# Which early store goes out in two halves of 64 partitions: row 1's, or that of rows 2 and 3

## The chip, the cores and the metric

The kernel runs on one core of a Trainium2 chip. The metric is device time in microseconds (us); a lower time is better. Differences under 2% count as "same". The profile is of one execution; its span, from the first to the last instruction, is about 1.7 us shorter than the timed run.

## The reference

Batch normalization with running statistics, then ReLU, on 32 x 128 x 32 x 32 float32 numbers, 16.78 MB in and 16.78 MB out:

```python
normalized = (x - running_mean[None, :, None, None]) / np.sqrt(running_var[None, :, None, None] + eps)
scaled = normalized * gamma[None, :, None, None] + beta[None, :, None, None]
return np.maximum(scaled, 0).astype(np.float32)
```

## The kernel before

The tensor is cut into two blocks t of 128 partitions x 16 rows x 1024 numbers; a row is one channel image of 4 KB in each partition. SyncE issues the six loads, ScalarE (ACT) computes each row in place with one activation (the first three rows of the second block with two), and issues the stores itself.

```python
TILES = ((0, 0, 2), (0, 2, 4), (0, 4, 16), (1, 0, 16))
LOAD_CUTS = {(0, 8), (1, 8)}
STORE_CUTS = {(0, 1)}
TWO_PARTS = {(0, 1)}
...
nc.sync.dma_start(out=xt[:, c - a : d - a, :], in_=xr[t, :, c:d, :])
...                                            # parameters: scale_t, bias_t
for t, a, b, xt in tiles:
    first = a
    for j in range(a, b):
        ...                                    # activation(s) of row j, Relu(scale * x + bias)
        if j + 1 == b or (t, j + 1) in STORE_CUTS:
            parts = P // 2 if (t, j) in TWO_PARTS else P
            for p in range(0, P, parts):
                nc.scalar.dma_start(out=outr[t, p : p + parts, first : j + 1, :],
                                    in_=xt[p : p + parts, first - a : j + 1 - a, :])
            first = j + 1
```

In order: row 0 (512 KB), row 1 in two halves (256 KB each), rows 2 and 3 (1 MB), rows 4 to 15 (6 MB), the second block (8 MB).

## Time and profile before

| | before |
|---|---|
| time, median of 3 runs | 83.4 us (83.33 to 83.64) |
| span of the profiled run | 81.7 us |
| ScalarE busy | 39.3 us (48%) |
| load queue q1 / store queue q10, share of 16 DMA engines | 48.6% / 47.7% |

Read the two shares first: they are packet time, that is, time in which a DMA engine moves a piece (packet) of a transfer, and they leave 3.7% of the span for everything that isn't a transfer. The prediction shows the lines.

### The profile page before, as it was taken

Reading aid. Unit: us, or ns where it says so; the run is one execution under the profiler, and the core shown is the slowest. Engines: PE = TensorE matmul, PEld = TensorE weight load, DVE = VectorE, ACT = ScalarE, POOL = GpSimd, SP = SyncE. Lnnn points to the kernel's source line nnn. Section 1 sums busy time; section 2 is a strip of 40 time slices with the busy share of each in tenths; the row PEclk is TensorE's granted clock in tenths of the full one; section 3 lists DMA queues with packets and bytes.
Section 4 is the critical chain, followed back from the end, with each engine's and each line's share of the span. In section 5 each row is a group of like instructions: output and inputs, shape, how many; then the busy total and the mean of one; then the engine's idle time right before and its main releaser. Section 6 shows DMA issues by size and latency. Waiting matters only on the chain.

```text
span 81.7 us, 129 instructions
## 1 busy us (share of the span) xinstructions
PE 1.8 (2%) x6; PEld 1.5 (2%) x6; DVE 0.8 (1%) x5; ACT 39.3 (48%) x37; POOL 0.8 (1%) x6
## 2 busy tenths in 40 slices
PE   0007000000000000000000000000000000000000
PEld 0016000000000000000000000000000000000000
DVE  0003000000000000000000000000000000000000
ACT  0601658797039999199998099994000000000000
POOL 3000000000000000000000000000000000000000
DMA  1999998898989799979789988889992899999290
GB/s 40 361 421 461 425 537 353 377 489 377 489 343 523 343 491 411 487 293 589 337 361 601 513 385 385 385 385 409 625 633 128 385 513 513 513 513 417 96 513 0
DMA packets 1665, 33.56 MB, mean 411 GB/s; under 512 B 257, under 2 KB 257, under 8 KB 513
## 3 DMA queue, kind: packets, MB, share of 16 engines
q1 hardware_dynamic: 864, 16.78, 48.6%
q10 hardware_dynamic: 800, 16.78, 47.7%
q14 instruction: 1, 0.00, 0.0%
HBM read 16.78 MB, written 16.78 MB: 411 GB/s over the span
## 4 chain that ended last, share of the span: by engine, by line
DMA 55%; ACT 10%; issue 2%; SPq 1%
DMA x<-in_x_dram 55%; ACT x L113 10%; SPq L58 1%
## 5 line engine op out<-in xcount | busy, mean ns | idle before, releaser
L113 ACT ACTIVATE x<-x,bias_t,scale_t 128x1024 f32<-128x1024 f32 (+1 forms) x35 | 37.8, 1154 | 11.4 <-DMA x<-in_x_dram 7.7
L95 ACT ACT_TABLE_LOAD x1 | 1.3, 1283 | 2.6 <-issue 2.6
L86 PE MATMUL cols<-raw,rep 8*128 8x16 f32 (+1 forms) x6 | 1.8, 384 | 6.3 <-DMA raw<-in_gamma_dram 6.0
L86 PEld LDWEIGHTS cols<-raw,rep 8*128 8x128 f32 x6 | 1.5, 306 | 6.5 <-issue 5.9
L95 ACT ACTIVATE std_t<-cols,eps_t 128x16 f32<-128x16 f32 x1 | 0.3, 273 | 2.7 <-PE cols L86 2.7
L72 POOL TENSOR_SCALAR_AFFINE_SELECT rep<-rep 8x128 f32<-8x128 f32 x1 | 0.4, 393 | 0.1
L99 DVE RECIPROCAL rstd_t<-std_t 128x16 f32<-128x16 f32 x1 | 0.3, 252 | 6.0 <-ACT std_t L95 6.0
L71 POOL MEMSET rep<- 8x128 f32 x1 | 0.2, 194 | 0.3 <-POOLq L144 0.3
L105 DVE TENSOR_TENSOR bias_t<-cols,ms_t 128x16 f32<-128x16 f32 x1 | 0.2, 175 | 0.4 <-PE cols L86 0.4
L103 DVE TENSOR_TENSOR ms_t<-cols,scale_t 128x16 f32<-128x16 f32 x1 | 0.2, 176 | 0.1
L101 DVE TENSOR_TENSOR scale_t<-cols,rstd_t 128x16 f32<-128x16 f32 x1 | 0.2, 175 | 0.1
L144 POOL MEMSET const-bfloat16-1.0<- 128x1 bf16 x1 | 0.1, 106 | 0.0
L144 POOL MEMSET const-uint8-127<- 128x1 uint8 x1 | 0.1, 106 | 0.0
L144 POOL MEMSET const-float32-0.0<- 128x1 f32 x1 | 0.1, 103 | 0.3 <-issue 0.3
L144 POOL MEMSET const-float32-1.0<- 128x1 f32 x1 | 0.1, 103 | 0.0
L69 DVE MEMSET eps_t<- 128x1 f32 x1 | 0.1, 59 | 0.9 <-PEq L144 0.9
## 6 DMA issues: line engine op xcount, KB each, us to landing
x<-in_x_dram SPq DMA_DIRECT2D x3, 4096.0 KB, 34.1
out_dram<-x ACTq DMA_DIRECT2D x1, 6144.0 KB, 28.5
x<-in_x_dram SPq DMA_DIRECT2D x2, 1024.0 KB, 5.6
x<-in_x_dram SPq DMA_DIRECT2D x1, 2048.0 KB, 11.1
out_dram<-x ACTq DMA_DIRECT2D x1, 1024.0 KB
out_dram<-x ACTq DMA_DIRECT2D x1, 512.0 KB, 14.4
out_dram<-x ACTq DMA_DIRECT2D x2, 256.0 KB, 19.2
raw<-in_running_var_dram ACTq DMA_DIRECT2D x1, 0.5 KB
```

The lines of the kernel that those rows point to most:

```text
L58: nc.sync.dma_start(out=xt[:, c - a : d - a, :], in_=xr[t, :, c:d, :])
L69: nc.vector.memset(eps_t, float(eps))
L71: nc.gpsimd.memset(rep, 1.0)
L72: nc.gpsimd.affine_select(out=rep, in_=rep, compare_op=mybir.AluOpType.is_equal, fill=0.0, base=0, pattern=[[0, P // Q], [-1, Q]], channel ...
L86: nc.tensor.matmul(c.rearrange("p k j -> p (k j)"), rep.rearrange("q r s -> q (r s)"), raw[a].rearrange("q k j -> q (k j)"), start=True, s ...
L95: nc.scalar.activation(out=std_t, in_=cols[0][:, 0, :], func=ACTF.Sqrt, bias=eps_t[:, 0:1], scale=1.0)
L99: nc.vector.reciprocal(out=rstd_t, in_=std_t)
L101: nc.vector.tensor_mul(out=scale_t, in0=cols[0][:, 1, :], in1=rstd_t)
L103: nc.vector.tensor_mul(out=ms_t, in0=cols[1][:, 0, :], in1=scale_t)
L105: nc.vector.tensor_sub(out=bias_t, in0=cols[2][:, 0, :], in1=ms_t)
L113: nc.scalar.activation(out=xt[:, j - a, w : w + step], in_=xt[:, j - a, w : w + step], func=ACTF.Relu, bias=bias_t[:, j : j + 1], scale=sc ...
L144: nc = _bacc.Bacc("TRN2", target_bir_lowering=False, num_devices=1)
```

## The change

The intent is to issue row 1 with one instruction, so that ScalarE comes to row 2 sooner, and to keep the number of transfers by splitting the next store.

```diff
-TWO_PARTS = {(0, 1)}
+TWO_PARTS = {(0, 3)}
```

## The prediction

> **What bounds the kernel now.** I read the page first, for which engine is full. ScalarE (ACT) does all the visible arithmetic and is busy for 48% of the span; TensorE, VectorE and GpSimd do next to nothing. The DMA engines are the ones with no holes.
>
> ```profile
> span 81.7 us, 129 instructions
> ...
> ACT  0601658797039999199998099994000000000000
> ...
> DMA  1999998898989799979789988889992899999290
> ...
> q1 hardware_dynamic: 864, 16.78, 48.6%
> q10 hardware_dynamic: 800, 16.78, 47.7%
> ...
> HBM read 16.78 MB, written 16.78 MB: 411 GB/s over the span
> ```
>
> Queue q1 carries the loads that SyncE issues, q10 the stores (and the tiny parameter loads) that ScalarE issues. Each percentage is packet time as a share of 16 engines over the span. Together they are 96.3%, and 0.963 x 81.7 = 78.7 us. The packet records of the trace (start, size and duration of each packet) begin at 1.8 us and the last one ends at 80.6 us, a stretch of 78.8 us. So an average engine stands still for about 0.1 us between its first packet and its last. The single digits below 9 in the DMA row come from packets being as long as a slice (one 32 KB packet takes 1.21 us, a slice is 2.04 us), not from idleness; a table of windows confirms it (columns: length of the stretch, five engines' busy times, clock, DMA share, GB/s):
>
> ```profile
> 13.00:24.00 11.00, 0.00 (x0) 0.00 (x0) 0.00 (x0) 6.65 (x7) 0.00 (x0) 1.00 1.01 429
> 24.00:36.00 12.00, 0.00 (x0) 0.00 (x0) 0.00 (x0) 10.31 (x10) 0.00 (x0) 1.00 1.03 437
> 36.00:46.00 10.00, 0.00 (x0) 0.00 (x0) 0.00 (x0) 8.71 (x10) 0.00 (x0) 1.00 0.94 404
> ```
>
> Row 0's store moves in the first of these, the two halves of row 1 in the second, rows 2 and 3 in the third. The shares (a packet is counted whole where it starts, so 1.03 and 0.94 are the same thing) average 1.00.
>
> Third, the chain that ended last. Its view stops at 56 us, because ScalarE's last instruction is its end; what comes after is seen in the waits of SyncE's queue, which sits through the stores until the program ends:
>
> ```profile
> SPq L158 <- DMA out_dram<-x: 67.6, 3, 34.0
> SPq L58 <- DMA x<-in_x_dram: 5.0, 1, 5.0
> SPq L58 <- DMA raw<-in_beta_dram: 4.7, 1, 4.7
> ```
>
> The last store's completion arrives at 80.9 us, then 0.8 us of closing. The other 1.7 us up to the 83.4 us of the timed runs lie outside the profiled span. So the kernel is 33.56 MB through 16 engines that are never idle, plus 4.6 us of fixed ends (1.8 before the first packet, 0.3 from the last packet to its completion, 0.8, and 1.7). Only a change in bytes, in time per byte, or in idle engine time can move it.
>
> Fourth, the timeline of ScalarE around the stores concerned (start, length, what; in brackets the engine's idle time before it):
>
> ```profile
> 9.60 0.39 ACTq L123 DMA_DIRECT2D out_dram<-x  x1
> 10.03 1.24 ACT L113 ACTIVATE x<-x,bias_t,scale_t 128x1024 f32<-128x1024 f32 x1 [0.46 <-ACT x L113]
> 11.30 1.18 ACTq L123 DMA_DIRECT2D out_dram<-x  x2
> 12.53 2.37 ACT L113 ACTIVATE x<-x,bias_t,scale_t 128x1024 f32<-128x1024 f32 x2 [1.26 <-issue]
> 14.93 0.38 ACTq L123 DMA_DIRECT2D out_dram<-x  x1
> 15.35 4.63 ACT L113 ACTIVATE x<-x,bias_t,scale_t 128x1024 f32<-128x1024 f32 x4 [0.46 <-ACT x L113]
> 23.88 9.16 ACT L113 ACTIVATE x<-x,bias_t,scale_t 128x1024 f32<-128x1024 f32 x8 [3.90 <-DMA x<-in_x_dram]
> ```
>
> Row 1's two issues take 1.18 us against 0.39 and 0.38 for a whole one. After row 7, at 19.98 us, ScalarE waits 3.90 us for the load of rows 8 to 15.
>
> **What the Trainium skill says.** "DMA: Bandwidth & Descriptors", Rules for kernel authors, says of two transfers to disjoint partition halves "Don't bother — they serialize"; the trace agrees: row 1's halves land at 30.5 and 36.1 us, one after the other. The same page, Queues, rings and completion order, says that each DMA engine takes turns between the queues that have work, a packet at a time. The packet records agree exactly: a 32 KB load packet of 1.213 us alternates with one store packet, 0.159 us for 4 KB or 0.309 us for 8 KB, and a 4-byte completion write takes a turn of its own. The page "SBUF — State Buffer", Door 1: The DMA port swizzle, says that 64 adjacent partitions reach only half of the 16 ports, at 196 GB/s against 328 for 128. That would speak against halves, but the trace doesn't show it here: in the packet records the 4 KB packets of row 1's halves take 159 ns, those of the whole row 0 take 159 to 160 on average. "Perfetto Trace Analysis", Roofline, puts a single core's ceiling at about 435 GB/s of its 16 engines; the trace has 33.56 MB in 78.8 us = 426 GB/s. There is no slack to win.
>
> **The change part by part.** The name in the code is the last row of a store, so row 1 (the transfer of 512 KB) becomes one of 128 partitions, and rows 2 and 3 (1024 KB) become two of 64 partitions with 8 KB each.
>
> Removed: one issue at row 1. Two take 1.18 us, one about 0.38, so row 2 starts near 11.30 + 0.42 = 11.7 us instead of 12.53, 0.8 us earlier; its load landed at 7.9 us, so nothing else holds it.
> Added: one issue after row 3, again about 1.18 in place of 0.38 us. Rows 2 and 3 end at 11.7 + 2.4 = 14.1, the issues at 15.3, and row 4 starts at 15.3 to 15.4 us, against 15.35 now. The two cancel. If they didn't, the 3.90 us wait before row 8 would take it up.
> DMA packets: row 1 stays 128 packets of 4 KB, 8 an engine (two times 4 before); rows 2 and 3 stay 128 of 8 KB, 8 an engine. The number of transfers stays six, so completion writes stay six times 16. Bytes, packet sizes and packets: change 0.
> Order in the store queue: an engine's turns are now 8+1 (row 0), 4+1 and 4+1 (row 1), 8+1 (rows 2 and 3), that is 28. They become 9, 9, 5, 5: again 28, beside the same load packets. Row 1 no longer spends a turn on a completion in its middle, so its end and the start of rows 2 and 3 come one load packet earlier: first 8 KB packets near 35.4 instead of 36.6 us. The completion between the halves gives the turn back, about 41.5 us. When the last load packet ends (46.4 us), seven of the eight 8 KB packets of an engine have gone, before and after. The load of the first rows of the second block (landing 34.7 us) may meet one more 4 KB packet: 0.16 us later, and ScalarE, which ends that block at 44.7 us, has 2.15 us of wait after it. So the last load still lands near 46.8, ScalarE ends near 56.0, and the last store is issued at 56.05 while the store before it is still moving until 61.2 us.
> Sum: 0.8 - 0.8 on ScalarE, off the path; 0.00 us on the DMA engines. Predicted 83.4 us.
>
> **The rivals.** First, crowded ports: if an 8 KB packet of a half took twice its time, eight packets an engine at 0.309 us more would add 2.5 us, 85.9 us in all (+3%). For it speaks the SBUF page; against it row 1's 159 ns. Only a small trace of it could be there: the load packets beside the first packets of row 1's second half take some 1.28 instead of 1.213 us, once per engine, under 0.1 us, and similar ones stand where no half begins.
> Second, completion semaphores: transfers share them in turn, which is why the SyncE queue waits 5.0 us (its last load waits for the load of rows 4 to 7). If the change shifted who shares with whom, a load might be held back. Against: the count of transfers, and row 1 now one fewer and rows 2 and 3 one more, leaves all later ones at their places; and the load queue has 8 MB before it at that point, so even a wait until row 0's store has landed (24.0 us) would starve nothing: 83.4 still.
> Third, an earlier ScalarE: starting row 2 0.8 us sooner might bring stores sooner and gain. Against: the store queue of each engine is backed up from 13.3 us on (row 0's packets move until 24 us), so an earlier issue only waits longer: 83.4.
> Fourth, a wobble in how the two queues interlock: the load packets' excess over 1.213 us sums to about 0.33 us an engine (29.46 us of packet time for 24 x 1.213 = 29.11). Redistributing it could give plus or minus 0.15 us.
>
> **Range and chances.** The three runs spread from 83.33 to 83.64. With that and the fourth rival, 83.15 to 83.75 should hold it 8 times in 10. A change of 2% is 1.7 us; only the first rival makes one, and the trace contradicts it for 4 KB packets; I leave 1.5% for it and half a percent for a gain that I don't see.
>
> **What would show it.** In the profile after: the two queues' packets still 864 and 800 with shares summing to 96 to 97%; row 2 starting near 11.7 and row 4 near 15.35 us; an issue pair of about 1.2 us after row 3; 8 KB packets still 0.309 us, the first near 35.4; last load landing 46.8, last store's completion 80.9 us. The prediction would be wrong if 8 KB packets of the halves took longer than 0.4 us, if a load stood behind a semaphore until the load queue was empty, or if the DMA share fell below 1 in a stretch between 13 and 80 us.

## The result, and the profile after

The changed kernel took 83.69 us (83.46 to 83.72, 6 runs) against 83.53 us (83.33 to 83.73, 6 runs) for the kernel before. The ratio is 1.0015, 95% interval 0.9995 to 1.0034: the same. A ratio here is the mean time of one kernel's fast runs over that of the other's of the same rounds, so it is not quite the ratio of the medians.

Lines of the page of the changed kernel that answer to those of before:

```profile
span 81.9 us, 129 instructions
...
DMA  2899999997979797979979988889997599999190
...
q1 hardware_dynamic: 864, 16.78, 48.5%
q10 hardware_dynamic: 800, 16.78, 47.6%
...
HBM read 16.78 MB, written 16.78 MB: 410 GB/s over the span
```

The packet counts and bytes of both queues are those of before, and the shares are within 0.1 point. By the packet records an average engine works for 78.76 us, against 78.67 us before, and stands still for 0.2 us between its first and last packet, against 0.1 us. The windows of the changed kernel (length, busy times of five engines, clock, DMA share, GB/s) say that the engines stay full through the stretches in which the early stores go out:

```profile
13.00:24.00 11.00, 0.00 (x0) 0.00 (x0) 0.00 (x0) 5.82 (x6) 0.00 (x0) 1.00 1.01 429
24.00:36.00 12.00, 0.00 (x0) 0.00 (x0) 0.00 (x0) 10.19 (x10) 0.00 (x0) 1.00 1.03 440
36.00:46.00 10.00, 0.00 (x0) 0.00 (x0) 0.00 (x0) 8.96 (x10) 0.00 (x0) 1.00 0.93 401
```

The timeline of the changed kernel around the edit (start, length, what, and in brackets the idle time before it):

```profile
8.21 0.33 SPq L58 DMA_DIRECT2D x<-in_x_dram  x1
...
11.39 0.37 ACTq L123 DMA_DIRECT2D out_dram<-x  x1
11.81 2.37 ACT L113 ACTIVATE x<-x,bias_t,scale_t 128x1024 f32<-128x1024 f32 x2 [0.45 <-ACT x L113]
14.21 1.18 ACTq L123 DMA_DIRECT2D out_dram<-x  x2
15.44 4.63 ACT L113 ACTIVATE x<-x,bias_t,scale_t 128x1024 f32<-128x1024 f32 x4 [1.26 <-issue]
24.06 9.16 ACT L113 ACTIVATE x<-x,bias_t,scale_t 128x1024 f32<-128x1024 f32 x8 [3.98 <-DMA x<-in_x_dram]
```

The 1.18 us pair of issues has moved from after row 1 to after row 3. Row 2 starts 0.72 us earlier, row 4 0.09 us later, and the wait before row 8 is what it was. The first line is a surprise: SyncE's last load goes out at 8.21 us, not at 12.77. The waits of SyncE's queue say why:

```profile
SPq L158 <- DMA out_dram<-x: 72.3, 3, 38.7
SPq L58 <- DMA raw<-in_beta_dram: 4.6, 1, 4.6
...
SPq L58 <- DMA x<-in_x_dram: 0.4, 1, 0.4
```

The 5.0 us wait of before is down to 0.4 us: the last load now waits for the load of rows 2 and 3 (landed at 8.19 us), no longer for that of rows 4 to 7. The transfers share eight completion semaphores, counters that tell the issuing engine that a transfer has landed; a transfer is issued only when the one that had its semaphore before has landed. With the edit the assignment changed, though the number of transfers did not: the last load and the 6 MB store swapped semaphores. Why the program's builder chose so, no run shows.

The span is 0.18 us longer in this one profile. At least part of that isn't of the change: the load of rows 0 and 1 already lands at 5.70 us in place of 5.38, before the first altered instruction.

### The profile page after: what moved, and what is told of

The parts are those of the page before. It is cut to its first block, busy times and chain, and to the rows that moved or that the text cites. A ratio compares the mean times of both kernels' runs of the same rounds, so it can differ in the third digit from the quotient of the medians.

```text
span 81.9 us, 129 instructions
## 1 busy us (share of the span) xinstructions
PE 1.7 (2%) x6; PEld 1.5 (2%) x6; DVE 0.8 (1%) x5; ACT 39.3 (48%) x37; POOL 0.8 (1%) x6
## 2 busy tenths in 40 slices
DMA packets 1664, 33.56 MB, mean 410 GB/s; under 512 B 256, under 2 KB 256, under 8 KB 512
## 4 chain that ended last, share of the span: by engine, by line
DMA 56%; ACT 10%; issue 2%; SPq 0%
DMA x<-in_x_dram 56%; ACT x L113 10%; SPq L58 0%
```

## The experiments

The theory: all 33.56 MB go through 16 DMA engines that are always busy; the edit alters neither bytes nor packets nor idle time, so neither the issues on ScalarE nor the place of the halves matter. The rivals: a half costs something of its own; ScalarE's issue time is on the path; the earlier last load hides a cost. Twelve runs were made, one of them a repeat of the changed kernel; all gave correct results. Times are medians; the kernel before ran beside them in each of three calls at 83.74, 83.55 and 83.73 us. By the 2% rule most of these runs are "the same"; the intervals of several leave out 1 all the same, and these small differences are discussed as such.

| run | edit | time us | ratio to before, 95% |
|---|---|---|---|
| after_again | the changed kernel | 83.62 | 0.999 (0.9975 to 1.0006) |
| no_halves | no store in halves | 84.30 | 1.007 (1.0053 to 1.0086) |
| both_halves | row 1 and rows 2 and 3 | 83.98 | 1.0043 (1.002 to 1.0066) |
| last_halves | row 1 and the last store | 103.40 | 1.2355 (1.2335 to 1.2374) |
| quarters | rows 2 and 3 in four | 84.07 | 1.0057 (1.0027 to 1.0087) |
| eighths | rows 2 and 3 in eight | 93.41 | 1.1179 (1.1148 to 1.1211) |
| busy_in_row2 | 5 us more ScalarE work early | 83.53 | 0.9997 (0.9979 to 1.0015) |
| busy_at_end | 10 us more ScalarE work late | 89.80 | 1.0751 (1.0724 to 1.0777) |
| row0_halves | row 0 alone in halves | 83.88 | 1.0023 (1.0007 to 1.0039) |
| rows01_halves | rows 0 and 1 in halves | 84.38 | 1.008 (1.0062 to 1.0099) |
| single_rows | no halves, rows 2 and 3 singly | 84.34 | 1.0076 (1.0061 to 1.0092) |
| pairs_whole | no halves, rows 0 and 1 in one | 92.89 | 1.1099 (1.1081 to 1.1117) |

**after_again.** No edit to the changed kernel; five rounds.

> The changed kernel unaltered, timed in five rounds, since 0.16 us lay between the medians and the interval touched 1. Theory (16 DMA engines always busy, same packets before and after, so no difference): ratio within 0.998 to 1.002 of before. Rival (a small real cost of the halves of rows 2 and 3, about 0.15 us): ratio 1.001 to 1.003 with an interval that leaves out 1.

Measured 83.62 us, ratio 0.999. With the first ratio of 1.0015 on the other side of 1, the theory's interval holds and no cost of 0.15 us is seen.

**no_halves, both_halves.** Against the kernel before:

```diff
-TWO_PARTS = {(0, 1)}
+TWO_PARTS = set()                 # no_halves
+TWO_PARTS = {(0, 1), (0, 3)}      # both_halves
```

> No store in halves: row 1 and rows 2 and 3 whole, one transfer and 16 completion writes fewer. Theory: 83.5 us, within 0.2 us of before; ScalarE issues 0.8 us less and only waits longer before row 8. Rival 1 (a half costs something): 0.15 us or more faster than the changed kernel. Rival 2 (ScalarE's issue time is on the path): 0.8 us faster.

> Row 1 and rows 2 and 3 both in halves: ScalarE issues 0.8 us more than either kernel, and the last load again shares a completion semaphore with the load of rows 4 to 7 (issued near 13 us, as in the kernel before, not near 8 us as in the changed one). Theory: 83.6 us, within 0.2 us of both. Rival 1 (halves cost): 0.15 us above the changed kernel. Rival 3 (the earlier issue of the last load in the changed kernel hid a cost of the halves): here the cost would come out, 0.3 us or more above the kernel before.

The theory missed both: 0.7% and 0.4% slower than before, where it said equal. Alone, both_halves would fit a cost of the halves (0.36 us above after_again) or a hidden one. But no_halves contradicts every rival: with less issue time, one transfer fewer and no half at all, it should have been equal or faster, and it is the slowest of the three. In both_halves the last load again waits until 12.75 us, as in the kernel before; but since no_halves is slow with an early last load (7.82 us), and the kernel before is fast with a late one, the time of that issue isn't what hides or makes a cost. Where the time went is taken up below, with the runs that were meant to explain it.

**last_halves.** The kernel before, with its last store in halves too.

```diff
-TWO_PARTS = {(0, 1)}
+TWO_PARTS = {(0, 1), (1, 15)}
```

> The kernel before with its last store of 8 MB in halves of 64 partitions as well. It moves alone at the end, so nothing hides what a half costs: this measures the disputed cost by itself. Theory (an engine's rate is its own, whatever partitions it reads): 64 KB packets stay 2.42 us, 83.6 us in all. Rival (64 partitions reach half of the ports): packets take about 4.8 us, eight an engine, so 19 us more, 103 us; then the halves of rows 2 and 3 were harmless only for being short and between load packets.

The rival hit: 103.4 us. Windows over the last store, first of the kernel before, then of this one (the last two figures are the DMA share and GB/s):

```profile
61.00:80.00 19.00, 0.00 (x0) 0.00 (x0) 0.00 (x0) 0.00 (x0) 0.00 (x0) 1.00 0.96 417
```

```profile
61.00:80.00 19.00, 0.00 (x0) 0.00 (x0) 0.00 (x0) 0.00 (x0) 0.00 (x0) 1.00 0.91 193
80.00:100.00 20.00, 0.00 (x0) 0.00 (x0) 0.00 (x0) 0.00 (x0) 0.00 (x0) 1.00 0.98 210
```

The engines are as busy as before and move half. In the packet records a 64 KB packet takes 5.11 us (median) in place of 2.418. A busy share alone can't tell a full engine from one that is held up; the GB/s beside it can. So a half of 64 partitions does cost double in a store of 8 MB that moves alone. In the changed kernel it doesn't: its 8 KB packets take 0.309 us, as in the kernel before, apart from four of the last 16, which come when the loads are ending and take 0.33 to 0.488 us. An engine's 8 KB packets add up to 2.50 us, against 2.47 us before.

**quarters, eighths.** The changed kernel with finer parts:

```diff
-parts = P // 2 if (t, j) in TWO_PARTS else P
+parts = P // 4 if (t, j) in TWO_PARTS else P     # quarters
+parts = P // 8 if (t, j) in TWO_PARTS else P     # eighths
```

> Rows 2 and 3 in four transfers of 32 partitions: twice the splits, 1.2 us more issue time than the changed kernel, and the last load now shares a completion semaphore with row 0's store, so it can't be issued before that lands at 24 us. Theory: the load queue holds work until 34 us and ScalarE's wait before row 8 shrinks from 4.0 to about 2.8 us, so 83.6 us, within 0.25 us of before. Rival (issue time or the shared semaphore on the path): 1.2 us more or beyond.

> Rows 2 and 3 in eight transfers of 16 partitions. Now the transfers share semaphores with stores that are still waiting in the queue: ScalarE can't issue the seventh before row 1's store has landed (35 us) nor the eighth before the second has, so rows 4 to 15 start near 37 us, and the last load must wait for the first eighth. Theory (only idle DMA engines cost time): engines stand idle between about 47 and 52 us and again before the last store, which is issued near 70 us; 93 us, 91 to 96. Rival (splits cost nothing whatever their number): 83.7 us.

In quarters the last load could not go out before 24.96 us, when row 0's store had landed, and still landed at 46.73 us. The wait cost nothing at the load. The time is 0.57% up, more than the 0.25 us expected and less than the rival's 1.2 us; it is one of the small misses treated below, where it stays unexplained for the most part. Eighths came out as expected, 93.4 us. Its timeline and its windows:

```profile
14.31 22.34 ACTq L123 DMA_DIRECT2D out_dram<-x  x8
36.70 13.68 ACT L113 ACTIVATE x<-x,bias_t,scale_t 128x1024 f32<-128x1024 f32 x12 [22.42 <-DMA out_dram<-x]
```

```profile
46.00:53.00 7.00, 0.00 (x0) 0.00 (x0) 0.00 (x0) 6.56 (x8) 0.00 (x0) 1.00 0.54 229
...
67.00:72.00 5.00, 0.00 (x0) 0.00 (x0) 0.00 (x0) 2.85 (x3) 0.00 (x0) 1.00 0.49 210
```

Eight issues take 22.34 us, because the fifth needs a semaphore that row 0's store holds until 24.8 us, and the seventh one that row 1's store holds until 35.8 us. ScalarE is held until 36.7 us, and the DMA share then falls to about a half twice. The shared semaphores of the prediction's second rival are a real cost, once the wait outlasts the queue.

**busy_in_row2, busy_at_end.** The changed kernel with idle work on ScalarE, four activations into a spare tile after row 2, or eight after row 14 of the second block:

```diff
+if (t, j) == (0, 2):              # busy_at_end: (1, 14), range(8)
+    for _ in range(4):
+        nc.scalar.activation(out=spare, in_=xt[:, j - a, :], func=ACTF.Relu, ...)
```

> The changed kernel with four more activations into a spare tile between rows 2 and 3, about 4.7 us of ScalarE work, six times what a split's issue costs. Theory: rows 4 to 7 end near 24.8 us, 0.8 us past the landing of the next load, and the wait near 35 us takes that up; 83.65 us, within 0.25 us of the changed kernel. Rival (ScalarE early in the kernel is on the path): up to 4.7 us more.

> The changed kernel with eight more activations before its last row, about 9.2 us, so that the last store is issued near 65.4 us instead of 56.2. Theory: the store before it drains at 61.4 us; the engines then stand idle until about 1 us after the issue, 66.4 us, so 5 us more, 88.7 us (88 to 89.5). This shows how much late ScalarE work is free: about 4 us. Rival (all ScalarE work is off the path): 83.7 us; rival (all of it is on the path): 92.9 us.

The early work, 5.06 us by the trace, is free: 83.53 us. The wait before row 8 is gone and the one near 35 us is 0.66 us, so nearly all slack there is used, and the time doesn't notice:

```profile
13.14 5.06 ACT L123 ACTIVATE spare<-x,bias_t,scale_t 128x1024 f32<-128x1024 f32 x4
...
34.93 1.52 ACT L114 ACTIVATE x<-x,bias_t,scale_t 128x512 f32<-128x512 f32 x2 [0.66 <-DMA x<-in_x_dram]
```

The late work took 10.15 us, a little more than I counted on (1.27 us an activation in place of 1.15), and cost 89.8 - 83.6 = 6.2 us. The time lies above the expected range of 88 to 89.5 us, mostly because the added work was longer; 10.15 - 6.2 = 4.0 us of it were free, as expected. The window of busy_at_end in which the engines wait for the last store, which is issued at 66.34 us:

```profile
61.00:66.50 5.50, 0.00 (x0) 0.00 (x0) 0.00 (x0) 5.21 (x5) 0.00 (x0) 1.00 0.00 0
```

A DMA share of 0.00 is what a cost on the path looks like in this kernel.

**row0_halves, rows01_halves, single_rows, pairs_whole.** These were to explain the 0.4 to 0.7% of no_halves and both_halves. My second theory was the number of turns that an engine takes in the store queue before the 6 MB store: 28 in the kernels before and after, 27, 29 and 30 in the slower ones.

```diff
-STORE_CUTS = {(0, 1)}
-TWO_PARTS = {(0, 1)}
+STORE_CUTS = {(0, 1)};          TWO_PARTS = {(0, 0)}             # row0_halves
+STORE_CUTS = {(0, 1)};          TWO_PARTS = {(0, 0), (0, 1)}     # rows01_halves
+STORE_CUTS = {(0, 1), (0, 3)};  TWO_PARTS = set()                # single_rows
+STORE_CUTS = set();             TWO_PARTS = set()                # pairs_whole
```

> Only row 0 in halves. The runs without halves (27 turns of each engine in the store queue before the 6 MB store), with both pairs (29) and with quarters (30) were 0.3 to 0.7% slower than before, the kernels before and after (28) were equal. Theory: what counts is the number of turns, not which row has the halves; here 28 again: ratio to before 0.998 to 1.002, about 83.6 us. Rival (the row matters): 0.3% or more off.

> Rows 0 and 1 in halves, rows 2 and 3 whole: 29 turns, like the run with row 1 and rows 2 and 3 in halves. Theory of the number of turns: ratio 1.003 to 1.006, about 84.0 us, and load packets near 43 us that take longer than 1.213 us. Rival (the halves of 8 KB packets made that run slower): ratio 0.998 to 1.002.

> No halves, but rows 2 and 3 in a store each of 4 KB packets: four early stores, 36 turns of 4 KB, so the loads end some 0.6 us earlier (near 46.1 us) and nine turns of row 3's store are left after them. If the slowness without halves came from the 48 KB packets of the next store standing close behind the last load packet, it must be gone here: ratio 0.998 to 1.002, about 83.6 us. If 28 is the only good number of turns: ratio 1.003 or more. If it came from having no halves at all: ratio 1.005 or more.

> No halves and rows 0 and 1 in one store like rows 2 and 3: 18 turns. The early stores are then through near 41 us, so the 48 KB packets of the 6 MB store come between the last four load packets (1.815 us each in place of 0.309): the last load lands near 54 us in place of 46.8, ScalarE ends near 63 us, the engines wait about 3 us for the last store, and the time is 86.9 us (86 to 88). Rival (only bytes count, in whatever order they go): 83.5 us.

Row0_halves has 28 turns and is 0.23% slower, with an interval that leaves out 1; rows01_halves has 29 turns and is at 0.8%, above its range; single_rows, with 36 turns, is at 0.76%, so the 48 KB packets behind the last load packet aren't the cause either; the two alternatives named there would fit, but both_halves and row0_halves are slow with halves, and row0_halves with 28 turns. The number of turns doesn't order these results: 28 turns gave 0.9990, 0.9997 and 1.0023 at the same number, and 29 gave 1.0043 and 1.008. That theory falls as I put it.

What the packet records do show is where most of the time sits. Per engine, the 24 load packets of 32 KB add up to:

| | before | after | after_again | no_halves | both_halves | row0_halves | rows01_halves | single_rows |
|---|---|---|---|---|---|---|---|---|
| us | 29.46 | 29.37 | 29.52 | 29.99 | 29.80 | 29.93 | 30.05 | 30.13 |
| above before | | -0.09 | 0.06 | 0.53 | 0.34 | 0.47 | 0.59 | 0.67 |

For no_halves, 0.53 us stand against (1.007 - 1) x 83.7 = 0.59 us in the timed runs; for both_halves 0.34 against 0.36; for single_rows 0.67 against 0.64. (One profile each; for row0_halves the profile has more than the timed 0.19 us.) The store packets' time moves by less than 0.1 us an engine among these runs, and the engines' idle time between first and last packet is 0.0 to 0.2 us in all of them. In no_halves, rows01_halves, row0_halves and single_rows most of it is in the last load packet of each engine: 1.35 to 2.0 us in place of 1.213. In the kernel before, the last load packets take 1.213 us; in the two profiles of the changed kernel one and three of the 16 take 1.28 to 1.375 us. In both_halves the longer packets are spread over the loading (0.15 us of their excess lie after 41 us).

Two things don't fit this account. Quarters is 0.49 us slower by its mean time, but its load packets take only 29.64 us, 0.18 above before. And part of the loss lies outside the profiled span: timed run less span is 1.73 us on average in the kernels before and after, but 1.88 us in no_halves, 1.90 in both_halves, 1.93 in rows01_halves and 1.85 in quarters. So these variants lose little in issue, in semaphores or in idle engines; for the most part load packets take longer. What stretches them, and what the rest is, stays open.

Pairs_whole was expected at 86.9 and came to 92.9 us. Its timeline after the loads, and the window in which the engines then stand idle:

```profile
60.13 9.16 ACT L113 ACTIVATE x<-x,bias_t,scale_t 128x1024 f32<-128x1024 f32 x8 [12.96 <-DMA x<-in_x_dram]
69.32 0.34 ACTq L123 DMA_DIRECT2D out_dram<-x  x1
```

```profile
61.00:64.00 3.00, 0.00 (x0) 0.00 (x0) 0.00 (x0) 3.00 (x4) 0.00 (x0) 1.00 0.00 0
```

The early stores landed by 38.7 us, not near 41; from there each load packet took turns with a 48 KB packet of 1.815 us. Six load packets of an engine and the load's completion write were still to come, (59.75 - 38.5) / (1.213 + 1.815) = 7 turns, where I had counted four load packets. The last load landed near 60.1 us and ScalarE's last rows had nothing to run beside. So order can matter after all: the small early store packets keep the large ones from coming between the loads. The edit in question leaves that guard as it is: eight 4 KB packets and eight of 8 KB for rows 1 to 3 on each engine, and three completions.

No run beat both kernels.

## Why the prediction was right

The time, 83.69 and later 83.62 us, lies in the range of 83.15 to 83.75, and "same" is what came. That it was so close is in part luck: the same reasoning gave 83.5 us for no_halves, which took 84.30, and nothing in the prediction tells the one edit from the other. What is shown is the bound and that the moved issues are free; "within 0.3 us" isn't.

*Bound.* Right. Only runs in which the DMA engines stood idle (busy_at_end, eighths, pairs_whole) or were held up (last_halves) lost more than 1%. Early ScalarE work of 5.06 us cost nothing.

*ScalarE's part.* Right within 0.1 us: row 2 at 11.81 us (predicted near 11.7), row 4 at 15.44 (15.3 to 15.4), pair of issues 1.18 us (about 1.18).

*Packets and turns.* Right: 864 and 800 packets; the first 8 KB packet at 35.43 us (35.4), the completion writes between the halves from 41.50 us on (about 41.5); the last load landed at 46.97 and in the second profile at 46.81 us (46.8), the last store's completion came at 81.09 and 80.99 us (80.9).

*Second rival, semaphores.* The step "leaves all later ones at their places" was wrong. The number of transfers stayed, but the builder's order did not, and the last load went out 4.56 us earlier. The second half of the argument carried the result: the load queue has work at that time, so an earlier or later issue doesn't show. Quarters holds the same load back to 24.96 us and it lands at 46.73 us; eighths shows where this ends.

*First rival, ports.* Its outcome was judged rightly for this kernel, on too general a reason. That row 1's packets took 159 ns did not mean that halves are free: in the 8 MB store of last_halves they take 5.11 against 2.418 us. Nor are load packets in between needed: in both_halves, 37 packets of 8 KB of a half start after the last load packet has ended, and 36 of them take 0.309 us. In eighths, after the last load packet before the gap ended at 35.16 us, 67 of the 68 that start before 36.6 us take 0.309 us; later ones take up to 1.246 us. So the loss shows in a long run and not in a short one. That data are read ahead would fit this, and would fit that the first 64 KB packets of last_halves took only 3.93 us on average; but no run separates it, so this is an argument and not shown. By the prediction's own sign (no 8 KB packet over 0.4 us), two of 128 packets were over it in the first profile of the changed kernel (0.465 and 0.488 us) and one in the second (0.571 us), which comes to less than 0.03 us an engine.

*Fourth rival, wobble.* The excess that it starts from is 29.46 - 29.11 = 0.35 us, not 0.33. Its size, 0.15 us, was short in general, though it held for this change. Neighbouring kernels differ by 0.2 to 0.8%, for the most part through load packets that take longer.

## What to carry to other kernels

When the packet time of the DMA queues fills the span, ask of an edit only whether it changes bytes, rate per packet, or idle engine time; moved issue instructions then cost nothing as long as the queues hold work. Read GB/s beside the DMA share, since engines that are held up look just as busy. A store of half the partitions that runs long and alone can take twice its time; measure it there and not in a short stretch. Small stores ahead of a large one can be a guard that lets the loads finish first, so before merging them work out what will stand between the last loads.

## What the Trainium skill lacked or had wrong

- "DMA: Bandwidth & Descriptors", Rules for kernel authors, advises against two transfers to disjoint halves because they serialize. It doesn't say that the cost depends on the stretch: next to nothing for 1 MB between load packets (8 KB packets of 0.309 us either way, but for a few), 19.7 us (103.40 - 83.74) for 8 MB that moves alone.
- "SBUF — State Buffer", Door 1: The DMA port swizzle, has 196 GB/s for 64 partitions and 328 for 128 at 1 MiB. Here, in transfers of 4 and 8 MB, it was 193 to 210 GB/s against 417, which agrees in kind; the page doesn't say that the loss can be absent in a short stretch (36 of 37 packets at 0.309 us in both_halves).
- "DMA: Bandwidth & Descriptors", Bandwidth, has a sentence by which the HBM side, at about 358 GB/s, binds transfers between HBM and SBUF, without the condition that the same section gives for that figure (both cores of a pair streaming). One core moved 33.56 MB in 78.8 us here, 426 GB/s.
- The same page, Queues, rings and completion order, tells of turns by packet. It doesn't say that a 4-byte completion write takes a whole turn, so that a split transfer lets one more load packet pass (first 8 KB packet at 36.6 us before, at 35.43 after).
- No page that I found has it that load packets of the same size can take 1.35 to 2.0 us in place of 1.213 at the end of the loading, in kernels that differ only in how the small stores beside them are cut (such kernels took 0.2 to 0.8% longer here).
